# Weight buffers in slots of 16 KB and 8 KB instead of eleven of 8 KB, with gate and up of an expert in one slot

## The chip, the cores and the metric

The kernel runs on one core of a Trainium2 chip. The metric is the device time of one launch in microseconds (us). Three runs before the change took 1690.86, 1692.18 and 1693.26 us; the median is 1692.18. A trace is one further execution under the profiler.

## The reference

The program is a block of two transformer layers over 256 latent tokens and 256 context tokens of width 1024. Each layer modulates its input by a conditioning vector, mixes tokens (layer 0: Fourier groups beside grouped-query attention; layer 1: neighbourhood attention with the context), normalizes, and then runs a mixture of experts. Layer 0 feeds 512 tokens to its experts, layer 1 only the 256 latent ones. What matters here, cut from the reference:

```
scores = jax.nn.sigmoid((h @ w_router).astype(jnp.float32))
_, idx = lax.top_k(scores + e_bias.astype(jnp.float32), TOP_K)     # 8 of 64 experts
...
def expert_block(args):
    tok, e = args
    xb = h_pad[tok]
    a = jax.nn.silu(xb @ w_gate[e]) * (xb @ w_up[e])               # 1024 -> 256, twice
    return a @ w_down[e]                                           # 256 -> 1024
...
routed = jnp.zeros((n_tok + 1, d), h.dtype).at[slot_tok].add(y)[:n_tok]
shared = (jax.nn.silu(h @ s_gate) * (h @ s_up)) @ s_down
return routed + shared
```

Every expert has 1 MB each of gate, up and down weights in float32. All 64 are read in both layers, whatever the routing.

## The kernel before, in words

An expert layer is a list of **jobs** of 128 slots (rows of tokens) each, cut into lanes of 32 columns of the array. A job holds one to three experts: a pair has two, a t in layer 1 has three (`"ptptspt3ptpt3ptptspt3ptptp"`, L77, one letter a job after the first two), an s one expert whose products are formed with its weights split in two parts (`gate_up3`, `down3`). Layer 0 has 43 jobs; a t there is two jobs that share an expert. Layer 1 has 28. A job is worked as gate_up (the token rows against gate and up, L1331 in layer 0 and L1324 in layer 1), an activation, a transposition, down (L1342), and a scatter. On TensorE and SP the order is the order of the code (`manual_schedule`); the other engines are filled in by a scheduler.

**Tokens.** In layer 0, tokens of a job are fetched by an indirect DMA on POOL (`gather`, L1432). The results go back in one of two ways: for the jobs of the range `sent` (L1200) POOL adds them by an accumulating indirect DMA to two arrays accd in HBM (`send`, L1503); the others are placed by matmuls against a one-hot matrix (`scatter`, L1521). Near the end of layer 0, `fetch` (L1510) reads accd back through SP as tiles named ad. `fold` (L1406) joins the sums with the residual and gives the function that adds late scatters.

**Weights.** All weights are loaded by SP in program order, so a load whose slot is still in use holds back everything queued behind it. Slots come from a pool; a slot is free again when the last reader of its tile has ended:

```
def w8(shape, name="w8", dt=F32):
    return wp.tile(shape, dt, name=name, tag="w8", bufs=11)
```

The eleven slots of 8 KB per partition hold, in turn, the modulation weights, the mixers' weights (`halves`, `load_wm`, `kv`), the shared expert (`sh`) and the experts. In layer 0, `load_gu` (L1039) makes two tiles of one expert, each with four of the eight row blocks of gate and up side by side, by four DMAs of 512 KB; one matmul gives gate and up in 512 columns. In layer 1 it makes a gate tile and an up tile, by one DMA of 1 MB each, and `gate_up` (L1318) first runs all gate matmuls (256 columns), then all up matmuls. `experts` (L1068) loads all first tiles of a job's new experts, then all second ones, then the downs. Some down weights of layer 1 go to other pools as dn and dnx (L1063). The first three experts of layer 0 and four of layer 1 are loaded before the routing is known (`static`); the rest are chosen by a register that SP loads from `ordi`.

The last job of layer 1 (`last_job`, L1575) runs gate, then pieces of the scatter, then up.

Of the kernel before, what the change touches and what calls it, by code (L numbers as in the profile page):

```python
# [114 lines left out]
def tile_block(ctx: ExitStack, tc: tile.TileContext, I, out):  # L115
# [79 lines left out]
    def load_wm(k):  # L195

        wm[k] = [w8([128, 4, 2, 256]) for _ in range(2)]
# [646 lines left out]
    def mixer_na(mp):  # L844
# [17 lines left out]
        def fill(n, steps):  # L862
# [8 lines left out]
            kv[n] = [w8([128, 4, 512], "kv") for _ in range(2)]  # L871
# [122 lines left out]
    def norm_h2(l, t, ps, rw_, mp):  # L994
# [17 lines left out]
        S.dma_start(h2d[t * 128:t * 128 + 128, :], hp.rearrange("t j p -> t (j p)"))  # L1012
# [21 lines left out]
    def moe(l, out_of, nt, mp, pre=lambda: None, post=lambda: None):  # L1034
# [4 lines left out]
        def load_gu(e, hs=(0, 1)):  # L1039

            if l:
                w = [w8([128, NJ, FF]) for _ in hs]
                for h, o in zip(hs, w):
                    S.dma_start(o, I[("moe_w_gate", "moe_w_up")[h]][l, e].rearrange("o (p j) n -> p (o j) n", j=NJ))
                return w
            w = [w8([128, 2, 4, FF]) for _ in hs]
            for h, o in zip(hs, w):
                for q, nm in enumerate(("moe_w_gate", "moe_w_up")):
                    S.dma_start(o[:, q], I[nm][l, e].rearrange("o (p j) n -> p (o j) n", j=NJ)[:, 4 * h:4 * h + 4])
            return w  # L1050

# [148 lines left out]
        sent = range(3, njob - 4, 2) if l == 0 else ()  # L1200
# [117 lines left out]
        def gate_up(xT, ws, segs, mid=lambda: None):  # L1318
            p = bank()
            if l:  # L1320
                for q in range(2):
                    for j in range(NJ):
                        for k, sl, kw in segments(segs):
                            T.matmul(p[sl, q * FF:q * FF + FF], xT(j, sl), ws[k][0][q][:, j], start=j == 0,  # L1324
                                     stop=j == NJ - 1, **kw)
# [669 lines left out]
```

## Time and profile before

| | |
|---|---|
| median of three runs | 1692.18 us (1690.86 to 1693.26) |
| the profiled execution's own time | 1695.05 us |
| its span in the trace | 1693.3 us |
| TensorE busy | 1572.6 us, 93% |
| VectorE, ScalarE, GpSimd busy | 784.8, 452.0, 162.9 us |
| mean granted TensorE clock | 0.977 |
| moved by SP's queue | 510.16 MB |
| moved by POOL's queue | 37.81 MB |

The expert jobs of layer 0 stand from about 290 to 955 us, the mixer of layer 1 to about 1150, the experts of layer 1 from 1191 to about 1660. A stage is read by three columns: how much of it TensorE is busy, what clock it was granted, and how busy the DMA engines were. Where TensorE is full and DMA is not, the stage is as long as its matmuls; where DMA is full and TensorE is not, as long as its loads.

### The profile page before, as it was taken

What the parts mean: (1) busy time and instruction counts of PE and PEld (TensorE: products, weight loads), DVE (VectorE), ACT (ScalarE), POOL (GpSimd) and SP (SyncE); (2) the same over time, 40 slices, a digit from 0 to 9 for tenths busy, and PEclk for the clock granted to TensorE, in tenths of its full rate; (3) what the DMA queues carried; (4) which work ended last, traced back from release to release, by engine and by line L of the source; (5) the groups of instructions that cost most, each with busy time, mean ns of one, the idle gap of its engine ahead of it and who ended that gap; (6) DMA issues with size and microseconds to landing.
All of it is one profiled execution on the core that took longest, in us unless ns stands there. A gap on an engine that the chain in (4) does not pass through costs nothing. (4 is left out here: it accounts for less than half of the span.)

```text
span 1693.3 us, 27425 instructions
## 1 busy us (share of the span) xinstructions
PE 1572.6 (93%) x10238; PEld 928.5 (55%) x10238; DVE 784.8 (46%) x2118; ACT 452.0 (27%) x896; POOL 162.9 (10%) x148
## 2 busy tenths in 40 slices
PE   5999999999999999999979799999999998989984
PEld 3765687445445444444434577856656555555542
DVE  2465594356556544435256733347343422223225
ACT  2456311113223223223121333331221211112111
POOL 1003200012111121112200100011000000000001
PEclk9999999999999999999989899999999999999998
DMA  9948866779999999999979855256879999999992
GB/s 328 331 162 299 299 215 212 267 271 371 363 395 341 400 387 398 387 337 389 355 283 408 313 207 199 100 209 262 326 295 420 418 419 419 419 419 419 420 419 107
DMA packets 140808, 549.76 MB, mean 325 GB/s; under 512 B 14288, under 2 KB 23008, under 8 KB 109056
## 3 DMA queue, kind: packets, MB, share of 16 engines
q1 hardware_dynamic: 128368, 510.16, 77.0%
q0 software_dynamic: 12304, 37.81, 7.6%
q8 instruction: 82, 1.34, 0.3%
q14 instruction: 54, 0.44, 0.1%
HBM read 532.63 MB, written 21.05 MB: 327 GB/s over the span
## 5 line engine op out<-in xcount | busy, mean ns | idle before, releaser
L1331 PE MATMUL bank<-w,xT 128*32 128x512 f32 (+2 forms) x1488 | 254.0, 602 | 4.2 <-DMA w<-in_moe_w_up_dram 4.2
L1324 PE MATMUL bank<-w,xT 128*32 128x256 f32 (+2 forms) x2560 | 220.1, 395 | 29.1 <-DMA w<-in_moe_w_up_dram 25.4
L1342 PE MATMUL bank<-w,aT 128*32 128x512 f32 (+2 forms) x1232 | 234.6, 597 | 2.0 <-ACT aT L1298 2.0
L1279 DVE SCALAR_TENSOR_TENSOR a<-s,wsl,bank 128x256 f32<-128x256 f32 x71 | 34.1, 480 | 415.3 <-ACT s L1278 415.3
L1324 PEld LDWEIGHTS bank<-w,xT 128*32 128x32 f32 (+2 forms) x2560 | 130.9, 124 | 116.4 <-DMA w<-in_moe_w_up_dram 33.9
L1521 PE MATMUL bank<-yy,ss 128*128 128x512 f32 x624 | 177.6, 410 | 1.3 <-DVE yy L157 1.0
L1278 ACT ACTIVATE s<-bank 128x256 f32<-128x256 f32 x71 | 27.3, 385 | 544.2 <-PE bank L1331 278.7
L1513 DVE TENSOR_TENSOR acc<-acc,bank 128x512 f32<-128x512 f32 x228 | 149.5, 683 | 45.5 <-PE bank L1521 42.8
L1331 PEld LDWEIGHTS bank<-w,xT 128*32 128x32 f32 (+2 forms) x1488 | 78.6, 125 | 161.0 <-issue 155.0
L1342 PEld LDWEIGHTS bank<-w,aT 128*32 128x32 f32 (+2 forms) x1232 | 67.8, 124 | 120.0 <-issue 106.1
L1521 PEld LDWEIGHTS bank<-yy,ss 128*128 128x128 f32 x624 | 107.4, 190 | 22.5 <-DVE yy L157 2.7
L157 DVE TENSOR_TENSOR yy<-bank,yy 128x512 fp32r<-128x512 f32 x104 | 71.4, 688 | 89.8 <-ACT yy L157 89.8
L157 ACT CAST yy<-bank 128x512 fp32r<-128x512 f32 x104 | 60.9, 586 | 176.6 <-PE bank L1342 158.8
L1432 POOL DMA_INDIRECT xg<-h2d,idx x43 | 51.5, 1198 | 418.4 <-DVE acc L1513 216.8
L157 DVE TENSOR_TENSOR wl<-half,wh 128x1024 fp32r<-128x1024 f32 x35 | 42.7, 1224 | 70.8 <-ACT wh L157 70.8
L1235 DVE TENSOR_SCALAR oh<-ib,pos 128x64 bf16<-128x64 bf16 (+3 forms) x428 | 68.7, 241 | 12.1 <-PE bank L1262 12.0
L161 PE MATMUL bank<-wh,hT 128*128 128x512 f32 x160 | 65.7, 411 | 2.7 <-ACT wh L157 2.1
L162 PE MATMUL bank<-wh,hT 128*128 128x512 f32 x160 | 63.5, 397 | 0.3 <-DVE hT L157 0.2
L163 PE MATMUL bank<-wl,hT 128*128 128x512 f32 x160 | 63.6, 397 | 0.0
L1472 PE MATMUL bank<-ohr,h2p 128*128 128x256 f32 x448 | 60.8, 289 | 0.0
L1472 PEld LDWEIGHTS bank<-ohr,h2p 128*128 128x128 f32 x448 | 55.3, 190 | 8.6 <-PE bank L1324 4.8
L1503 POOL DMA_INDIRECT accd<-yd,idx x32 | 50.2, 1569 | 96.7 <-issue 90.7
(366 smaller groups left out, 2287.7 us busy)
## 6 DMA issues: line engine op xcount, KB each, us to landing
w<-in_moe_w_down_dram SPq DMA_DIRECT2D x104, 1024.0 KB
w<-in_moe_w_gate_dram SPq DMA_DIRECT2D x128, 512.0 KB
w<-in_moe_w_up_dram SPq DMA_DIRECT2D x128, 512.0 KB
w<-in_moe_w_gate_dram SPq DMA_DIRECT2D x64, 1024.0 KB
w<-in_moe_w_up_dram SPq DMA_DIRECT2D x64, 1024.0 KB
w<-in_w_mod_dram SPq DMA_DIRECT2D x24, 1024.0 KB
half<-in_na_w_in_dram SPq DMA_DIRECT2D x12, 1024.0 KB
mh<-in_w_mod_dram SPq DMA_DIRECT2D x12, 1024.0 KB
```

The source lines that it names most:

```text
L157: return A.copy(o_h, src), eng.tensor_sub(o_l, src, o_h.bitcast(F32))
L161: T.matmul(p, xh, wh, start=first, stop=False)
L162: T.matmul(p, xl, wh, start=False, stop=False)
L163: T.matmul(p, xh, wl, start=False, stop=last)
L1235: V.tensor_scalar(oh[:, 32 * lane:32 * (lane + m)], ib[:, off:off + 32 * m], pos[:, t, c:c + 1], None, op0=OP.is_equal)
L1324: T.matmul(p[sl, q * FF:q * FF + FF], xT(j, sl), ws[k][0][q][:, j], start=j == 0, stop=j == NJ - 1, **kw)
L1331: T.matmul(p[sl], xT(j, sl), ws[k][0][j // 4][:, :, j % 4, :], start=j == 0, stop=j == NJ - 1, **kw)
L1342: T.matmul(p[sl], aT[:, j, sl], d[:, n * 512:n * 512 + 512], start=j == 0, stop=j == 1, **kw)
L1432: G.indirect_dma_start(out=x, out_offset=None, in_=h2d[:n2, :], in_offset=bass.IndirectOffsetOnAxis(ap=idx_col, axis=0), bounds_check=n2 - ...
L1472: T.matmul(o, h2p[t][k][:, 2 * q + j], oh[:, t].rearrange("p a b -> p (a b)")[:, :n], start=t == 0 and k == 0, stop=t == nt - 1 and k == 1)
L1513: add = {0: lambda t, r, p: V.tensor_add(acc[t][:, r], acc[t][:, r], p)}
L1521: T.matmul(p, ss[:, t * 128:t * 128 + 128], yy[:, q, r], start=k == 0 and q == 0, stop=k == len(grp) - 1 and q == 1)
```

## The change

The pool of weight slots becomes four of 16 KB and three of 8 KB per partition. A 16 KB slot holds the gate and up weights of one expert (`gu`), or two halves of a mixer's weights, or the shared expert's gate and up. Both layers load an expert's gate and up by two DMAs of 1 MB and run gate_up with 512 columns. Down weights, modulation weights and biases stay in the 8 KB slots. The last job keeps gate before up, as `gate_then_up`. Besides: the write of h2d moves from SP to POOL, the range `sent` ends two jobs earlier (job 37 is scattered by matmuls), and `fold` treats only the latent tokens, with late context sums added to acc by VectorE.

```diff
     def w8(shape, name="w8", dt=F32):
-        return wp.tile(shape, dt, name=name, tag="w8", bufs=11)
+        return wp.tile(shape, dt, name=name, tag="w8", bufs=3)
+
+    def w16(shape, name="w16", dt=F32):
+
+        w = wp.tile([128, 2] + shape, dt, name=name, tag="w16", bufs=4)
+        return [w[:, 0], w[:, 1]]
 
     def halves(name="half", dt=F32):
 
-        return [w8([128, 4, 512], name, dt) for _ in range(2)]
+        return w16([4, 512], name, dt)
...
-        S.dma_start(h2d[t * 128:t * 128 + 128, :], hp.rearrange("t j p -> t (j p)"))
+        G.dma_start(h2d[t * 128:t * 128 + 128, :], hp.rearrange("t j p -> t (j p)"))
...
+        def load_gu(e):
+
+            w = wp.tile([128, 2, NJ, FF], F32, name="gu", tag="w16", bufs=4)
+            for q in range(2):
+                load_half(w, q, e)
             return w
+
+        def load_half(w, q, e):
+            S.dma_start(w[:, q], I[("moe_w_gate", "moe_w_up")[q]][l, e].rearrange("o (p j) n -> p (o j) n", j=NJ))
...
-            for c in new:
-                have[c] = [[], None]
-            for h in range(2):
-                for c, e in zip(new, es):
-                    have[c][0].extend(load_gu(e, (h,)))
+            for c, e in zip(new, es):
+                have[c] = [load_gu(e), None]
...
-        sh = []
-        for nm in ("sh_w_gate", "sh_w_up"):
-            w = w8([128, NJ, FF])
+        sh = w16([NJ, FF], "sh")
+        for w, nm in zip(sh, ("sh_w_gate", "sh_w_up")):
             S.dma_start(w, I[nm][l].rearrange("(p j) n -> p j n", j=NJ))
-            sh.append(w)
...
-        sent = range(3, njob - 4, 2) if l == 0 else ()
+        sent = range(3, njob - 6, 2) if l == 0 else ()
...
-                    T.matmul(p[sl], xT(j, sl), ws[k][0][j // 4][:, :, j % 4, :], start=j == 0, stop=j == NJ - 1, **kw)
+                    T.matmul(p[sl], xT(j, sl), ws[k][0][:, :, j, :], start=j == 0, stop=j == NJ - 1, **kw)
...
-            for t in range(nt):
-                V.tensor_mul(acc[t], acc[t], g2s[t // 2])
+            for t in range(2):
+                V.tensor_mul(acc[t], acc[t], g2s[0])
                 V.tensor_add(xt[t], xt[t], acc[t])
             g2c.extend(g2s[1:])
-            first = set()
 
             def add_x(t, r, p):
                 if t > 1:
-                    if (t, r.start) in first:
-                        return V.tensor_add(acc[t][:, r], acc[t][:, r], p)
-                    first.add((t, r.start))
-                    if r.start == 0:
-                        acc[t] = k4([128, D], "accx")
-                    return A.copy(acc[t][:, r], p)
+                    return V.tensor_add(acc[t][:, r], acc[t][:, r], p)
                 tmp = k2([128, 512], "tmp")
                 V.tensor_mul(tmp, p, g2s[0][:, r])
-                (G if r.start else V).tensor_add(xt[t][:, r], xt[t][:, r], tmp)
+                (G if l and r.start else V).tensor_add(xt[t][:, r], xt[t][:, r], tmp)
...
-                n_grp = 1 if sent and 2 < j < njob - 4 else GRP
+                n_grp = 1 if sent and 2 < j < njob - 6 else GRP
```

In the rows below, a row is one instruction that SP issues, in order; the names are the tile written and the array read, with buffer numbers, and "waits" names the semaphores it stands for: PE_49 is TensorE's count, a DMAHW or DMASW one an earlier DMA's.

First, SP at the start of layer 0's experts, before: the shared expert's weights stand ahead of the token tiles x0 to x3.

```order
L1090 DMA w8_1801<-in_sh_w_gate_dram 128x2048 [waits DMAHW4_49,DMAHW1_49,PE_49]
L1080 DMA cst_1793<-in_cols0_dram 128x128 [waits DMASW0_49,DVE_49,DMASW1_49,Activation_49,Pool_49]
L1082 DMA jm_1795<-in_jmask0_dram 128x129
L1086 DMA rb_1799<-in_moe_bias_dram 128x64
L1090 DMA w8_1803<-in_sh_w_up_dram 128x2048 [waits DMAHW2_49,PE_49]
L1084 DMA rw_1797<-in_moe_w_router_dram 128x512
L1054 DMA w8_1805<-in_sh_w_down_dram 128x2048 [waits DMAHW3_49,PE_49]
L213 DMA x0_1843<-in_x_dram 128x1024
```

And now:

```order
L1056 DMA w8_1793<-in_sh_w_down_dram 128x2048 [waits DMAHW4_49,DMAHW1_49,PE_49]
L1079 DMA cst_1782<-in_cols0_dram 128x128 [waits DMASW0_49,DVE_49,DMASW1_49,Activation_49,Pool_49]
L1081 DMA jm_1784<-in_jmask0_dram 128x129
L1085 DMA rb_1788<-in_moe_bias_dram 128x64
L218 DMA x0_1831<-in_x_dram 128x1024
L1083 DMA rw_1786<-in_moe_w_router_dram 128x512 [waits PE_49]
L218 DMA x1_1889<-in_x_dram 128x1024 [waits DMAHW2_49]
L218 DMA x2_1974<-in_ctx_dram 128x1024 [waits DMAHW3_49,PE_49,Activation_49]
L218 DMA x3_2078<-in_ctx_dram 128x1024 [waits DMAHW4_49,DMASW2_49,DVE_49]
L1088 DMA sh_1790<-in_sh_w_gate_dram 128x2048 [waits DMAHW5_49,PE_49]
L1088 DMA sh_1790<-in_sh_w_up_dram 128x2048 [waits DMAHW6_49]
```

Gate and up of the shared expert have moved behind the token tiles, into one tile sh, and the gate waits for TensorE there; the down weights stay in front.

Second, SP in the last pair job that stands ahead of the first ad, before: half tiles, then two downs, then ad, then the next (split) expert.

```order
L1049 DMA w8_7734<-in_moe_w_gate_dram 128x1024 [waits DMAHW3_49,PE_49]
...
L1049 DMA w8_7734<-in_moe_w_up_dram 128x1024 [waits DMAHW4_49]
...
L1049 DMA w8_7743<-in_moe_w_up_dram 128x1024 [waits DMAHW2_49]
...
L1054 DMA w8_7746<-in_moe_w_down_dram 128x2048 [waits DMAHW3_49,PE_49]
...
L1054 DMA w8_7748<-in_moe_w_down_dram 128x2048 [waits DMAHW4_49,PE_49]
L1510 DMA ad_7828<-accd0_77 128x1024 [waits DMAHW5_49,DMASW7_49,DMASW1_49]
L1510 DMA ad_7831<-accd1_78 128x1024 [waits DMAHW6_49,DMASW2_49]
...
L1049 DMA w8_7843<-in_moe_w_gate_dram 128x1024 [waits DMAHW7_49,PE_49]
...
L1049 DMA w8_7843<-in_moe_w_up_dram 128x1024 [waits DMAHW0_49]
```

And now, at the same place:

```order
L1052 DMA gu_7547<-in_moe_w_gate_dram 128x2048 [waits DMAHW7_49]
...
L1052 DMA gu_7547<-in_moe_w_up_dram 128x2048 [waits DMAHW0_49]
...
L1052 DMA gu_7550<-in_moe_w_gate_dram 128x2048 [waits DMAHW1_49,PE_49]
...
L1052 DMA gu_7550<-in_moe_w_up_dram 128x2048 [waits DMAHW2_49]
...
L1056 DMA w8_7553<-in_moe_w_down_dram 128x2048 [waits DMAHW3_49,PE_49]
...
L1056 DMA w8_7555<-in_moe_w_down_dram 128x2048 [waits DMAHW4_49,PE_49]
L1504 DMA ad_7635<-accd0_76 128x1024 [waits DMAHW5_49,DMASW1_49]
L1504 DMA ad_7638<-accd1_77 128x1024 [waits DMAHW6_49,DMASW5_49,DMASW2_49]
...
L1052 DMA gu_7650<-in_moe_w_gate_dram 128x2048 [waits DMAHW7_49]
...
L1052 DMA gu_7650<-in_moe_w_up_dram 128x2048 [waits DMAHW0_49]
```

Two whole experts take four DMAs of twice the size; the pair's second down (w8_7555) waits for TensorE directly ahead of ad, and the expert behind is gu_7650.

Third, SP at the start of layer 1's experts, before: three static experts after the first, with an h2d write between.

```order
L1044 DMA w8_10194<-in_moe_w_gate_dram 128x2048 [waits DMAHW3_49]
L1044 DMA w8_10195<-in_moe_w_up_dram 128x2048 [waits DMAHW4_49,PE_49]
L1054 DMA dn_10198<-in_moe_w_down_dram 128x2048 [waits DMAHW5_49]
L1044 DMA w8_10200<-in_moe_w_gate_dram 128x2048 [waits DMAHW6_49,PE_49]
L1044 DMA w8_10201<-in_moe_w_up_dram 128x2048 [waits DMAHW7_49,PE_49]
L1054 DMA dn_10204<-in_moe_w_down_dram 128x2048 [waits DMAHW0_49]
L1044 DMA w8_10206<-in_moe_w_gate_dram 128x2048 [waits DMAHW1_49,PE_49]
L1044 DMA w8_10207<-in_moe_w_up_dram 128x2048 [waits DMAHW2_49,PE_49]
L1054 DMA dn_10210<-in_moe_w_down_dram 128x2048 [waits DMAHW3_49]
L1012 DMA h2d_122<-hp_10239 128x1024 [waits DMAHW4_49,DVE_49]
```

And now:

```order
L1052 DMA gu_9698<-in_moe_w_gate_dram 128x2048 [waits DMAHW1_49,PE_49]
L1052 DMA gu_9698<-in_moe_w_up_dram 128x2048 [waits DMAHW2_49]
L1056 DMA dn_9701<-in_moe_w_down_dram 128x2048 [waits DMAHW3_49]
L1052 DMA gu_9976<-in_moe_w_gate_dram 128x2048 [waits DMAHW4_49,PE_49]
L1052 DMA gu_9976<-in_moe_w_up_dram 128x2048 [waits DMAHW5_49]
L1056 DMA dn_9979<-in_moe_w_down_dram 128x2048 [waits DMAHW6_49]
L1052 DMA gu_9981<-in_moe_w_gate_dram 128x2048 [waits DMAHW7_49,PE_49]
L1052 DMA gu_9981<-in_moe_w_up_dram 128x2048 [waits DMAHW0_49]
L1056 DMA dn_9984<-in_moe_w_down_dram 128x2048 [waits DMAHW1_49]
L1052 DMA gu_9986<-in_moe_w_gate_dram 128x2048 [waits DMAHW2_49,PE_49]
L1052 DMA gu_9986<-in_moe_w_up_dram 128x2048 [waits DMAHW3_49]
L1056 DMA dn_9989<-in_moe_w_down_dram 128x2048 [waits DMAHW4_49]
```

The four static experts stand in the same order, gate and up of each in one tile; the gate of each waits for TensorE once, the up no more, and the h2d write is gone from this queue.

## Rows read from the trace of the kernel before

**Rows 1.** The page, busy time of the engines: us, share of span, instructions.
```profile
PE 1572.6 (93%) x10238; PEld 928.5 (55%) x10238; DVE 784.8 (46%) x2118; ACT 452.0 (27%) x896; POOL 162.9 (10%) x148
```
**Rows 2.** Windows: stretch, us, each engine's busy us (instructions), PEclk, DMA share, GB/s.
```profile
400.00:800.00 400.00, 386.79 (x2378) 188.19 (x2377) 208.17 (x514) 112.10 (x192) 72.84 (x53) 1.00 1.00 377
...
1192.00:1253.00 61.00, 57.86 (x488) 36.00 (x485) 23.27 (x102) 13.59 (x25) 0.00 (x0) 1.00 0.80 318
1253.00:1655.00 402.00, 372.93 (x3425) 222.16 (x3425) 116.80 (x349) 73.34 (x143) 0.00 (x0) 0.98 1.01 418
```
**Rows 3.** The page's groups of gate_up: count | busy us, mean ns | idle before.
```profile
L1331 PE MATMUL bank<-w,xT 128*32 128x512 f32 (+2 forms) x1488 | 254.0, 602 | 4.2 <-DMA w<-in_moe_w_up_dram 4.2
L1324 PE MATMUL bank<-w,xT 128*32 128x256 f32 (+2 forms) x2560 | 220.1, 395 | 29.1 <-DMA w<-in_moe_w_up_dram 25.4
```
**Rows 4.** Waits of TensorE, 800 to 960 us: total us, times, longest.
```profile
PE bank L161 <- ACT wh L157: 5.4, 1, 5.4
...
PE bank L1331 <- DMA w<-in_moe_w_up_dram: 4.2, 3, 2.6
```
**Rows 5.** Waits of TensorE, 1190 to 1670 us.
```profile
PE bank L1324 <- DMA w<-in_moe_w_up_dram: 25.4, 16, 2.3
```
**Rows 6.** SP's issues, 186 to 200 us: start us, us, engine line op, tiles.
```profile
188.15 0.34 SPq L1090 DMA_DIRECT2D w<-in_sh_w_gate_dram  x1
...
191.68 0.33 SPq L1090 DMA_DIRECT2D w<-in_sh_w_up_dram  x1
```
**Rows 7.** TensorE, 241 to 254 us: start us, us, line, tiles, count.
```profile
242.72 0.39 PE L163 MATMUL bank<-wo,yT 128*128 128x512 f32 x1
...
244.68 7.13 PE L1379 MATMUL bank<-w,h2T 128*128 128x256 f32 x32
```
**Rows 8.** TensorE, 812 to 829 us: two jobs' gate_up and a down.
```profile
813.83 7.08 PE L1331 MATMUL bank<-w,xT 128*32 128x512 f32 x64
...
827.52 1.94 PE L1331 MATMUL bank<-w,xT 128*64 128x512 f32 x8
```
**Rows 9.** SP's issues, 820 to 900 us.
```profile
847.51 2.38 SPq L1510 DMA_DIRECT2D ad<-accd  x2
...
851.25 0.34 SPq L1049 DMA_DIRECT2D w<-in_moe_w_up_dram  x1
...
868.73 0.81 SPq L1510 DMA_DIRECT2D ad<-accd  x2
```
**Rows 10.** TensorE, 833 to 862 us.
```profile
837.65 3.65 PE L1342 MATMUL bank<-w,aT 128*64 128x512 f32 x16
...
848.51 1.18 PE L1521 MATMUL bank<-yy,ss 128*128 128x512 f32 x4
...
860.29 0.80 PE L161 MATMUL bank<-wh,xT 128*128 128x512 f32 x1 [5.42 <-ACT wh L157]
```
**Rows 11.** ScalarE, 853 to 863 us.
```profile
859.19 1.99 ACT L157 CAST wh<-w 128x1024 fp32r<-128x1024 f32 x2 [3.69 <-DMA w<-in_moe_w_up_dram]
```
**Rows 12.** Windows: the stretch right after that wait (columns of rows 2).
```profile
860.29:865.50 5.21, 5.17 (x11) 3.64 (x12) 4.70 (x4) 2.88 (x3) 0.00 (x0) 0.50 0.47 197
```
**Rows 13.** TensorE, 876 to 888 us.
```profile
881.10 7.33 PE L1331 MATMUL bank<-w,xT 128*32 128x512 f32 x44 [2.62 <-DMA w<-in_moe_w_up_dram]
```
**Rows 14.** VectorE, 932 to 946 us, one of the four L1410 adds.
```profile
937.74 1.22 DVE L1410 TENSOR_TENSOR xr<-xr,acc 128x1024 f32<-128x1024 f32 x1
```
**Rows 15.** SP's issues, 1145 to 1200 us.
```profile
1161.07 0.42 SPq L1054 DMA_DIRECT2D dn<-in_moe_w_down_dram  x1
...
1192.10 0.35 SPq L1054 DMA_DIRECT2D w<-in_moe_w_down_dram  x1
```
**Rows 16.** TensorE, 1191 to 1215 us: gate_up of layer 1's first two jobs.
```profile
1191.29 14.03 PE L1324 MATMUL bank<-w,xT 128*64 128x256 f32 x128
```
**Rows 17.** SP's issues, 1196 to 1262 us: x2 stands for two in one row.
```profile
1226.75 17.62 SPq L1044 DMA_DIRECT2D w<-in_moe_w_gate_dram  x2
```

More of the change, by code (lines that the diff above doesn't have):

```diff
@@ L195, in load_wm @@
     def load_wm(k):
-        wm[k] = [w8([128, 4, 2, 256]) for _ in range(2)]
+        wm[k] = w16([4, 2, 256], "wm")
         for h in range(2):
@@ L870, in fill @@
                 A.activation(qT[n][:, i], ps[i][:, :256], AF.Copy, scale=SCALE)
-            kv[n] = [w8([128, 4, 512], "kv") for _ in range(2)]
+            kv[n] = w16([4, 512], "kv")
             ps = project(na[2 + n], channel_major(h, 512), tick, nxt=lambda: na[4 + n])
@@ L1037, in moe @@
         NS = pl.ahead
[L1039 to L1049, printed above, removed]
-            return w
+        def load_gu(e):
+            w = wp.tile([128, 2, NJ, FF], F32, name="gu", tag="w16", bufs=4)
+            for q in range(2):
+                load_half(w, q, e)
+            return w
+        def load_half(w, q, e):
+            S.dma_start(w[:, q], I[("moe_w_gate", "moe_w_up")[q]][l, e].rearrange("o (p j) n -> p (o j) n", j=NJ))
         def load_dn(d_ap, tile=w8):
@@ L1316, in segments, with gate_up, gate_then_up @@
             return out
-        def gate_up(xT, ws, segs, mid=lambda: None):
+        def gate_up(xT, ws, segs):
             p = bank()
[L1320 to L1325, printed above, removed]
-                    if q == 0:
-                        mid()
-                return p
             for j in range(NJ):
                 for k, sl, kw in segments(segs):
-                    T.matmul(p[sl], xT(j, sl), ws[k][0][j // 4][:, :, j % 4, :], start=j == 0, stop=j == NJ - 1, **kw)
+                    T.matmul(p[sl], xT(j, sl), ws[k][0][:, :, j, :], start=j == 0, stop=j == NJ - 1, **kw)
+            return p
+        def gate_then_up(xT, ws, segs, mid):
+            p = bank()
+            for q in range(2):
+                for j in range(NJ):
+                    for k, sl, kw in segments(segs):
+                        T.matmul(p[sl, q * FF:q * FF + FF], xT(j, sl), ws[k][:, q, j], start=j == 0,
+                                 stop=j == NJ - 1, **kw)
+                if q == 0:
+                    mid()
             return p
@@ L1352, in gu_parts @@
                 wh, wl = k4(shape, "wh", F32R), k4(shape, "wl", F32R)
-            split(wh, wl, w[0][jj // 4][:, :, jj % 4:jj % 4 + 2], V)
+            split(wh, wl, w[0][:, :, jj:jj + 2], V)
             return wh, wl
@@ L1575, in last_job @@
             es = [ds(S.value_load(ordi[0:1, sg_[0]:sg_[0] + 1], min_val=0, max_val=NE - 1), 1) for sg_ in segs]
-            wgu = [[], []]
-            for h in range(2):
+            wgu = [wp.tile([128, 2, NJ, FF], F32, name="gu", tag="w16", bufs=4) for _ in es]
+            for q in range(2):
                 for w, e in zip(wgu, es):
-                    w.extend(load_gu(e, (h,)))
+                    load_half(w, q, e)
             wd = [w8([128, 2, D]) for _ in es]
@@ L1590, in two_pieces @@
                 next(sc)
-            p = gate_up(xT, [[w] for w in wgu], segs, two_pieces)
+            p = gate_then_up(xT, wgu, segs, two_pieces)
             for _ in sc:
```

## The prediction

> **What bounds the kernel now.** I read the engine line first: TensorE is busy for 1572.6 us of 1693.3 [rows 1]. That alone would say that only TensorE work counts, so I next read the stages [rows 2]. From 400 to 800 us (layer 0's experts) TensorE is busy for 386.79 us of 400 and the DMA engines are at 1.00 as well, at 377 GB/s: two resources are full at once and neither has slack for the other. From 1253 to 1655 us (layer 1's experts) the DMA share is 1.01 at 418 GB/s and TensorE has idle time. The waits agree: in layer 1, L1324 waits 25.4 us for weights in 16 pieces [rows 5], while layer 0's whole tail has one large wait, 5.4 us at L161, and 4.2 us at L1331 [rows 4]. So the reader is to see a kernel that lives on weights being loaded far ahead, and in layer 1 one that is as long as its weight stream. The change rearranges the buffers that hold this lead. The bytes of buffer stay 88 KB per partition; what differs is that seven slots, not eleven, are handed back, and gate and up of an expert together.
>
> **The change, part by part.** The sum is made against the profiled execution, 1695.05 us (span 1693.3 and 1.75 around it); the median of the runs is 2.87 lower, and I take that off at the end. 1 MB below is 1024 KB, 1.049 million bytes, so 2.51 us at 418 GB/s.
>
> *Matmul form.* In layer 1, 256-column matmuls become 512-column ones. L1331 spends 254.0 us on 1488 x 512 columns, L1324 220.1 us on 2560 x 256 [rows 3]: 0.333 and 0.336 ns a column, so 1.6 us of TensorE time is saved, in a stretch that waits for DMA. I count 0. The covering work is the weight stream; if it were gone, the gain would be 1.6.
>
> *Entry of layer 0, about +4.5 (0 to 6.5).* Before, the shared expert's gate and up were queued at 188 to 192 us [rows 6], some 50 us before L1379 reads them at 244.68 [rows 7]. Now all four 16 KB slots hold the output projection of the mixer until its last matmul, 242.72 + 0.39 = 243.1 [rows 7], and only then SP can issue the gate. It needs 2.51 us of transfer and a latency. The nearest row for that: the half expert queued at 851.25 reached ScalarE at 859.19, 7.9 us later, with 2.1 million bytes (5.0 us) to move from the first ad read before it [rows 9, 11], so at most 2.9 us. 243.1 + 2.5 + 2.6 = 248.2, against 244.68: 3.5 us of waiting. The up half follows 2.5 us later and is needed after half of the 7.13 us. I add 1 for the modulation streams, which now share three slots (0 to 2). The x loads and h2d writes change queue or place by a few microseconds and are waited for by nobody at the edge; 0.
>
> *Steady layer 0, about +7 (0 to 31).* A pair job lasts 13.69 us, 813.83 to 827.52 [rows 8], and brings six tiles, 15.1 us of DMA. A job with two new experts is short by 1.36 us, and the lead pays for it. With three down slots, SP now stands at a pair's second down load until the down matmuls of the job before have ended (the second fence of order rows on the tail shows such a PE wait just ahead of ad); behind it stand the next gate and up. Eight jobs of layer 0 bring two new experts right after a job that did: 8 x 1.36 = 10.9. Some of it is still covered, since two whole experts are loaded: I take 7. The lower end is that all is covered, as it is now; the upper counts the 0.5 MB gather and 0.5 MB scatter of each such job too, 8 x (1.36 + 2.5).
>
> *Tail of layer 0, about +4.5 (-5 to +9).* Before, SP stood until 847.51 at the read of ad, for an accumulating scatter that is now not sent; the split expert behind it was issued at 850 and TensorE waited 5.42 us at 860.29 [rows 9, 10]. That reason goes. What is late next: the second down load of the pair ahead of ad waits for the down matmuls that ended at 837.65 + 3.65 = 841.3 [rows 10]. From there two downs, two ad reads (0.5 MB each) and the gate and up, 5 MB or 12.6 us with what is in flight, and the latency give 856 to 858, against 854.9, when TensorE is free: a wait of about 2.4, so -3. The next job's weights are still issued behind the standstill to 868.73 [rows 9]; now its first matmuls want 4 MB, where half an expert each was enough. Two ad and 4 MB from 868.73 are 12.6 us, with latency 884, where the gate_up now goes through its last wait at 881.10 [rows 13]: +3.5. Sixteen more scatter matmuls, at 1.18 us for four [rows 10], less what overlaps: +4. -3 + 3.5 + 4 = +4.5.
>
> *Vector work at the end of layer 0: 0 (-2 to +2).* Two L1410 adds of 1.22 us leave the chain [rows 14], four adds of a bank to acc take their place.
>
> *Entry of layer 1 and its stream, about +14 (1.5 to 24).* Before, four static experts were queued by 1161.07 and SP took up the routed ones at 1192.10 [rows 15]; their weights fed 14.03 us of gate_up without a gap from 1191.29 [rows 16]. Now the fourth expert's gate and up need a slot that is freed only by the end of the first gate_up, 1191.29 + 14.03 / 2 = 1198.3, and the down loads that went at 1192.10 stand behind them. So the stream starts 6.2 us later and with 3 MB (7.5 us) still to bring: 13.7 us. From 1253 on, DMA is full at 1.01 [rows 2], so this lag reaches the end one for one. TensorE's own wait for the fourth expert, 5.0 us of transfer and a latency, lies inside it. Between 1192 and 1253 the DMA share is 0.80: 12.2 us are idle, around SP's standstill from 1226.75 to 1244 [rows 2, 17]. If all of it were taken up, 1.5 remains; if the third down slot adds about 10 us of standing there, 24. I expect one to replace the other.
>
> Sum: 4.5 + 7 + 4.5 + 0 + 14 = 30. 1695.05 + 30 = 1725; less 2.87, **1722**.
>
> **Two rules against the rows.** Layer 0 loads in pieces of 512 KB at 377 GB/s beside gathers and scatters, layer 1 in pieces of 1 MB at 418 [rows 2]. The Trainium skill, "DMA: Bandwidth & Descriptors", section on measured bandwidth, says to batch transfers to 1 MiB or more; by that rule layer 0's stream would come nearer to 418, the +7 would vanish and the time be 1715. After 5.42 us without work TensorE ran at 0.50 of its clock, 1.2 GHz, from 860.29 to 865.5 [rows 10, 12]. The Trainium skill, "TensorE: Matmul & The Clock Gate", section on HAM oscillation, tells of just this after waits for DMA; by it each new wait as long as that one costs 2.6 us more, and if three of mine were that long the sum would be 1730.
>
> **The rivals.**
> 1. *The lead is enough in layer 0.* For it: now TensorE waits almost nowhere there, and the bytes of buffer are the same. Against it: a DMA share of 1.00 over 400 us. Without the steady +7 and with half of the entry and tail (4.5), 1695.05 + 18.5 - 2.87 = 1711.
> 2. *Faster.* The one mechanism is the tail's standstill at ad: if its end lets the split expert and the next job load in time, the 5.4 and 4.2 us of waits and 2.6 us of half clock go [rows 4, 12], 12.2 in all, against 4 for the scatter matmuls: 1692.18 - 8.2 = 1684. It decides only if layer 1's stream also catches up its lag between 1198 and 1253, where it has 12.2 idle us for 13.7.
> 3. *The ring of four starves layer 1 all along.* A gate slot now comes free at the end of a gate_up, 3.5 us later than before (half of 7.0). Ten jobs of layer 1 have three experts and need a fifth slot with the next job. If half of the 3.5 is not covered each time, 10 x 1.75 = 17.5 us more: 1740. Against it: down loads are queued between, and keep the engines busy meanwhile.
> 4. *Nothing to be measured*: loss and gain cancel, 1692. No row speaks for a balance so exact.
>
> **How the numbers follow.** The forecast has 0.58, rival 1 has 0.18, rival 2 has 0.07, rival 3 has 0.14, rival 4 has 0.03. 0.2% (3.4 us) is about what a measurement of this kernel can tell from no change. All cases but rivals 2 and 4 are slower by more: 0.90; faster 0.07; the same 0.03. The forecast's own terms, none at its end, give 1710 to 1735; with rival 1 below and most of rival 3 above, the range is 1704 to 1738.
>
> **What would show it.** Right: a TensorE wait of 2 to 5 us at the shared expert's first matmul near 245; SP standing at down loads in layer 0, waits at gate_up on up weights; no 5.4 us wait at L161 but one of 2 to 3; a wait of about 6 us at layer 1's second gate_up; the DMA share from there to the end again 1.0 at 418 GB/s, but ending some 14 us later relative to layer 1's start. Wrong: layer 0 without DMA waits at gate_up (then rival 1), a first weight of the fourth expert that is issued before the first gate_up ends, or bubbles in the DMA share after 1270 (then rival 3).

## The result and the profile after

The changed kernel takes 1740.95 us (median of four, 1739.17 to 1743.61) against 1692.72 of the kernel before beside it: ratio 1.0286, interval 1.0272 to 1.03. It is 48.2 us slower, outside the range that was forecast (1704 to 1738). Its profiled execution has a span of 1739.2 us, 45.9 more than before.

The page's busy line answers [rows 1]: TensorE is busy for 26 us more, although it has 1236 instructions fewer.

```profile
PE 1598.8 (92%) x9002; PEld 886.1 (51%) x9002; DVE 786.0 (45%) x2118; ACT 451.4 (26%) x893; POOL 159.1 (9%) x150
```

Fixed stretches of time, as in [rows 2], hold other work in the two kernels, so I cut both traces at the same five instructions: a transposition in an early job of layer 0, a product of a split expert near its end, one of layer 1's mixer, a transposition of its routing, and a gather product further on (a matmul that fetches a job's tokens); the last stretch ends 17.1 us before the end of either span. A "..." stands for the mixer. Columns are those of rows 2. Before, the stretches are the steady part of layer 0, its tail, the start of layer 1's experts, and the rest of them:

```profile
321.30:797.00 475.70, 461.37 (x2848) 226.59 (x2846) 246.60 (x636) 132.46 (x228) 85.45 (x62) 1.00 0.97 362
797.00:961.40 164.40, 142.02 (x745) 69.83 (x743) 88.09 (x127) 40.24 (x71) 16.16 (x14) 0.93 0.90 337
...
1177.30:1343.00 165.70, 162.53 (x1428) 102.75 (x1427) 67.19 (x286) 35.34 (x66) 0.00 (x0) 0.99 0.86 348
1343.00:1676.20 333.20, 299.98 (x2667) 175.67 (x2666) 96.72 (x239) 61.38 (x119) 3.30 (x2) 0.97 0.96 398
```

The same work in the changed kernel:

```profile
325.83:819.46 493.63, 470.40 (x2844) 232.19 (x2843) 246.50 (x632) 132.80 (x228) 85.30 (x62) 0.98 0.91 349
819.46:984.82 165.36, 146.31 (x760) 75.15 (x758) 87.82 (x131) 37.17 (x66) 9.27 (x10) 0.92 0.88 343
...
1200.20:1388.60 188.40, 171.91 (x996) 84.41 (x995) 67.14 (x286) 35.30 (x66) 0.00 (x0) 0.96 0.82 335
1388.60:1722.10 333.50, 302.68 (x1851) 139.96 (x1850) 96.68 (x239) 61.40 (x119) 3.30 (x2) 0.96 0.95 390
```

Read the second column, the length. The entry gives 325.83 - 321.30 = +4.5, the steady part +17.9, the tail +1.0, the mixer 1200.20 - 1177.30 less what was there at 984.82 - 961.40, -0.5, the start of layer 1 +22.7, the rest +0.3: together 45.9. Two places carry 40.6 of it. In the steady part, half is idle TensorE (475.70 - 461.37 = 14.3 before, 23.2 now: +8.9) and half is the same matmuls running longer (+9.0), at a mean granted clock of 0.98 where it was 1.00. The DMA engines, at 0.97 before, are at 0.91. The start of layer 1 divides in the same way: +13.3 of idle time (3.17 before, 16.49 now) and +9.4 of longer matmuls, at 0.96 for 0.99.

The queue of loads tells why. SP's longest waits in layer 0 (400 to 860, the steady part and the first of the tail; total, times, longest), L1056 the downs and L1052 gate and up:

```profile
SPq L1056 <- PE bank L1342: 126.7, 13, 14.9
SPq L1056 <- PE bank L1259: 115.8, 11, 15.6
SPq L1056 <- DVE wl L162: 62.8, 7, 12.4
SPq L1052 <- PE bank L1319: 29.0, 9, 5.7
```

Before (400 to 850), the longest of those for TensorE, L1054 the downs and L1049 gate and up:

```profile
SPq L1054 <- PE bank L1331: 59.2, 15, 13.3
SPq L1049 <- PE bank L1331: 39.4, 23, 3.4
...
SPq L1049 <- PE bank L1262: 29.3, 8, 4.7
SPq L1049 <- PE bank L1342: 27.8, 8, 4.5
```

Before, SP stood for a slot for 88 us at the downs in all (59 in the row shown) and for about 100 at gate and up; now it stands for 305 us at the downs, with the next gate and up behind them, and for 35 at gate and up. TensorE meets this as a handful of new waits of 1.3 to 2.6 us: some 5 us more at split experts, whose weights need a copy (L162) before the product, and 3.9 us in two waits of pair jobs for up weights. One of the first kind and the granted clock with it, first on TensorE's timeline (in brackets the idle time ahead):

```profile
528.99 0.50 PE L166 MATMUL bank<-wh,xT 128*128 128x512 f32 x1 [1.37 <-ACT wh L162]
...
530.77 0.80 PE L168 MATMUL bank<-wl,xT 128*128 128x512 f32 x1 [1.04 <-DVE wl L162]
...
533.92 0.63 PE L166 MATMUL bank<-wh,xT 128*128 128x512 f32 x1
```

And the stretch at half clock in the windows:

```profile
530.10:536.90 6.80, 6.13 (x14) 4.81 (x15) 4.01 (x4) 1.68 (x2) 0.00 (x0) 0.50 1.02 425
```

The clock fell to 0.50, 1.2 GHz, at 530.1, within the second of two waits of 1.37 and 1.04 us, both shorter than the 5.42 of [rows 10, 12]. There are five such stretches between 400 and 800, 20 us in all; before there was one of 3.4 us. By an estimate from these numbers, 20 us at half the clock lose some 10 us of matmul time and the 3.4 before lost 1.7, which is most of the +9.0. Not every such wait does this: one of 1.65 us in the same kernel left the clock at 1.00.

```profile
612.84 0.50 PE L168 MATMUL bank<-parts,xT 128*128 128x512 f32 x1 [1.65 <-DVE parts L162]
```
```profile
612.84:619.00 6.16, 5.78 (x29) 4.56 (x29) 4.21 (x6) 3.49 (x6) 5.09 (x3) 1.00 1.03 412
```

The entry, SP and then TensorE [rows 6, 7]: the shared expert's gate is issued only when the output projection is all but done (its last matmul starts at 243.07), and its first product waits.

```profile
242.57 0.33 SPq L1088 DMA_DIRECT2D sh<-in_sh_w_gate_dram  x1
```
```profile
247.99 8.20 PE L1379 MATMUL bank<-sh,h2T 128*128 128x256 f32 x24 [2.39 <-DMA sh<-in_sh_w_gate_dram]
```

The tail of layer 0, SP and TensorE [rows 9, 10, 13]: the standstill is now at the downs ahead of ad, the 5.42 us wait has become 1.63, and the next job waits 6.3 us in two waits, where it waited 4.2 in three [rows 4].

```profile
850.09 14.69 SPq L1056 DMA_DIRECT2D w<-in_moe_w_down_dram  x2
864.89 0.96 SPq L1504 DMA_DIRECT2D ad<-accd  x2
866.63 0.34 SPq L1052 DMA_DIRECT2D gu<-in_moe_w_gate_dram  x1
```
```profile
879.61 0.50 PE L166 MATMUL bank<-wh,xT 128*128 128x512 f32 x1 [1.63 <-ACT wh L162]
...
899.33 1.93 PE L1319 MATMUL bank<-gu,xT 128*32 128x512 f32 x6 [3.29 <-DMA gu<-in_moe_w_up_dram]
904.31 2.74 PE L1319 MATMUL bank<-gu,xT 128*32 128x512 f32 x9 [3.05 <-DMA gu<-in_moe_w_up_dram]
```

The start of layer 1 [rows 15, 16]: SP takes the fourth expert's gate only at 1221.38, 7.1 us into the first gate_up, and the second gate_up waits. Over the whole layer TensorE's waits on up weights are 39.7 us, against the 25.4 of [rows 5], to which 3.6 for gates come. The surplus is all in the start: 13.3 us of such waits there, where there was none before.

```profile
1186.83 0.58 SPq L1056 DMA_DIRECT2D dn<-in_moe_w_down_dram  x1
1221.38 0.33 SPq L1052 DMA_DIRECT2D gu<-in_moe_w_gate_dram  x1
```
```profile
1214.27 7.94 PE L1319 MATMUL bank<-gu,xT 128*64 128x512 f32 x34
1228.80 7.56 PE L1319 MATMUL bank<-gu,xT 128*64 128x512 f32 x24 [6.58 <-DMA gu<-in_moe_w_up_dram]
```
```profile
PE bank L1319 <- DMA gu<-in_moe_w_up_dram: 39.7, 13, 6.6
```

### The profile page after: what moved, and what is told of

It reads as the page before. It is cut to its first block, busy times and chain, and to the rows that moved or that the text cites. A ratio compares the mean times of both kernels' runs of the same rounds, so it can differ in the third digit from the quotient of the medians.

```text
span 1739.2 us, 24323 instructions
## 1 busy us (share of the span) xinstructions
PE 1598.8 (92%) x9002; PEld 886.1 (51%) x9002; DVE 786.0 (45%) x2118; ACT 451.4 (26%) x893; POOL 159.1 (9%) x150
## 5 line engine op out<-in xcount | busy, mean ns | idle before, releaser
L1319 PE MATMUL bank<-gu,xT 128*32 128x512 f32 (+2 forms) x2736 | 481.1, 626 | 49.9 <-DMA gu<-in_moe_w_up_dram 49.9
L1319 PEld LDWEIGHTS bank<-gu,xT 128*32 128x32 f32 (+2 forms) x2736 | 153.5, 127 | 346.1 <-issue 328.1
L1515 PE MATMUL bank<-yy,ss 128*128 128x512 f32 x640 | 181.3, 410 | 1.9 <-DVE yy L162 1.6
L162 DVE TENSOR_TENSOR yy<-bank,yy 128x512 fp32r<-128x512 f32 x106 | 72.8, 688 | 94.0 <-ACT yy L162 94.0
L162 ACT CAST yy<-bank 128x512 fp32r<-128x512 f32 x106 | 61.9, 585 | 184.3 <-PE bank L1342 167.0
L162 DVE TENSOR_TENSOR wl<-half,wh 128x1024 fp32r<-128x1024 f32 x35 | 42.6, 1223 | 70.8 <-ACT wh L162 70.8
L1232 DVE TENSOR_SCALAR oh<-ib,pos 128x64 bf16<-128x64 bf16 (+3 forms) x428 | 68.5, 239 | 13.0 <-PE bank L1259 12.8
L1440 PEld LDWEIGHTS bank<-head,xg 128*128 128x128 f32 x344 | 39.5, 142 | 28.7 <-issue 26.8
L1440 PE MATMUL bank<-head,xg 128*128 128x128 f32 x344 | 53.2, 278 | 0.0
## 6 DMA issues: line engine op xcount, KB each, us to landing
gu<-in_moe_w_up_dram SPq DMA_DIRECT2D x128, 1024.0 KB, 13.9
```

The lines of the kernel that those rows point to most:

```text
L162: return A.copy(o_h, src), eng.tensor_sub(o_l, src, o_h.bitcast(F32))
L1232: V.tensor_scalar(oh[:, 32 * lane:32 * (lane + m)], ib[:, off:off + 32 * m], pos[:, t, c:c + 1], None, op0=OP.is_equal)
L1319: T.matmul(p[sl], xT(j, sl), ws[k][0][:, :, j, :], start=j == 0, stop=j == NJ - 1, **kw)
L1440: T.transpose(p[:, j * 128:j * 128 + 128], x[:, (q * 4 + j) * 128:(q * 4 + j) * 128 + 128], ident)
L1515: T.matmul(p, ss[:, t * 128:t * 128 + 128], yy[:, q, r], start=k == 0 and q == 0, stop=k == len(grp) - 1 and q == 1)
```

## The experiments

**The queue changes alone.** On the kernel before: h2d from POOL, the shorter range `sent`, the new `fold`; the eleven slots stay.

```diff
-        S.dma_start(h2d[t * 128:t * 128 + 128, :], hp.rearrange("t j p -> t (j p)"))
+        G.dma_start(h2d[t * 128:t * 128 + 128, :], hp.rearrange("t j p -> t (j p)"))
...
-        sent = range(3, njob - 4, 2) if l == 0 else ()
+        sent = range(3, njob - 6, 2) if l == 0 else ()
...
```

> The kernel before with only the other parts of the change: h2d written by POOL, the sent jobs ending two earlier, the shorter fold. Eleven slots of 8 KB stay. Theory (the slots alone cost the 48 us): SP no longer stands at ad until 847, so most of the 5.4 us wait at the split job goes, for 4 us of scatter matmuls: 1687 to 1692. Rival (these parts carry some of the loss): 1697 or more.

1692.48 us, ratio 0.9994 (0.9982 to 1.0006): no difference that can be measured, and just above the range of the theory (1687 to 1692). Together these parts carry none of the loss; it belongs to the slots and what goes with them. That the parts cancel each other is shown by the last run below.

**Layer 0: the downs behind the next gate and up.** The changed kernel, with SP's order in layer 0 turned: before a job's downs, the next job's gate and up are queued.

```diff
...
+                if l == 0:
+                    gate_ups([sg_[0] for sg_ in segs])
+                    if j + 1 < njob:
+                        gate_ups([sg_[0] for sg_ in jobs[j + 1]])
+                    downs([sg_[0] for sg_ in segs])
...
```

> The changed kernel, in layer 0 with one other order on SP: gate and up of the next job are queued ahead of the down weights of this one. Theory A (in layer 0 SP standing at the three down slots holds back the next gate and up, and the waits and half clock come from that): the lag against before at the end of layer 0's steady part falls from about 22 us to 8 to 12, the end to 1726 to 1732. Rival B (four slots of gate and up, or the bandwidth beside gathers and scatters, are the limit): 1738 to 1745, with waits for down weights instead.

1723.43 us, ratio to before 1.0174 (1.0153 to 1.0194): 17.5 less than the changed kernel, more than the theory asked. The lag at the end of the steady part fell less than it asked, from 22.5 to 15.7 us instead of 8 to 12, in part because this trace entered the steady part 3.7 us later than the changed kernel's; the tail gave the rest. The two stretches of layer 0:

```profile
329.51:812.69 483.18, 464.34 (x2843) 230.46 (x2841) 247.99 (x635) 132.34 (x228) 81.81 (x62) 0.99 0.95 364
812.69:966.12 153.43, 138.59 (x760) 72.21 (x760) 86.69 (x128) 38.74 (x67) 9.09 (x9) 0.97 0.92 360
```

The steady part loses 7.5 us against before where it lost 17.9, and the tail is 11.0 shorter than before: with gate and up ahead of the standstill the waits of [rows 4] go as well. SP stands no shorter in this run, 398 us from 321 to 835 against 391 in the changed kernel:

```profile
SPq L1052 <- PE bank L1333: 283.7, 28, 17.6
```

but now mostly at gate and up. So the standing by itself was not the cost; what was queued behind it was.

**A fourth 8 KB slot, and its control.** Room for a fourth slot comes from the pool of 4 KB tiles; the control has that cut alone.

```diff
-NK4 = 13
+NK4 = 11
...
-        return wp.tile(shape, dt, name=name, tag="w8", bufs=3)
+        return wp.tile(shape, dt, name=name, tag="w8", bufs=4)
```

> Control for the next run: the changed kernel with the pool of 4 KB tiles cut from 13 to 11 buffers, to make room for one more 8 KB slot. Theory: these buffers are spare, 1739 to 1744. Rival (they are needed): over 1746.

> The changed kernel with a fourth 8 KB slot (and the pool of 4 KB tiles cut as in the control). Theory (layer 0's loss is SP standing for a down slot of the ring of three, with the next gate and up behind it): layer 0 regains most of what the other order of loads gave, so 10 to 17 us less than the control. Rival (a ring of four hands a pair's slots back just as late, because the same down matmuls free them two by two): within 5 us of the control.

The control takes 1810.5 us (1.0689, 1.0665 to 1.0712): its rival was right, those tiles are needed (42.9 us late at 961, 114 at the end). So only the difference counts: with the slot 1790.78 us (1.0575, 1.0559 to 1.0592), 19.7 less, somewhat more than the 10 to 17 of the theory. The steady part of layer 0, the control first, then with the fourth slot:

```profile
336.25:831.95 495.70, 470.35 (x2844) 232.31 (x2842) 247.60 (x632) 133.39 (x228) 85.78 (x62) 0.98 0.91 349
```
```profile
336.31:818.16 481.85, 461.80 (x2843) 226.14 (x2842) 247.20 (x632) 133.29 (x228) 85.77 (x62) 1.00 0.95 363
```

The control has the changed kernel's loss here (495.70 against 493.63), and one slot takes 13.9 us of it away, most of the 9 us of longer matmuls among them (470.35 to 461.80). By size and by order the same cause is shown: the ring of three down slots holds back gate and up. Neither repair takes all: 6 to 7.5 us stay in the steady part. With the fourth slot nearly all of them are idle time (20.05 us against 14.33 before). No run shows what they come from; four slots for gate and up, or loads of 1 MB where there were 512 KB, are untested rivals.

**Layer 1: gates in one slot, ups in another.** The changed kernel, with two experts' gates loaded into one 16 KB slot and their ups into the next, and all gate matmuls ahead of the ups, 256 columns each.

```diff
...
+                w = [wp.tile([128, 2, NJ, FF], F32, name="gu", tag="w16", bufs=4) for _ in range(2)]
+                for q in range(2):
+                    for k, (c, e) in enumerate(cc):
+                        S.dma_start(w[q][:, k], I[("moe_w_gate", "moe_w_up")[q]][l, e].rearrange(
+                            "o (p j) n -> p (o j) n", j=NJ))
...
```

> The changed kernel, in layer 1 with one slot for two experts' gates and one for their ups, gates loaded and multiplied first (256 columns), so that a slot is handed back after half a gate_up. Number and size of slots stay. Theory A (the 9 us that the stream of layer 1 loses after its late start come from slots that are handed back 3.5 us later): DMA share back to 1.0 from 1276 on, 1730 to 1734. Rival B (four slots of 16 KB are too few in either form): 1738 to 1745.

1728.19 us (1.0206, 1.0191 to 1.0222), 12.8 less than the changed kernel and below both ranges. It changes two things at once, the slots' contents and the form of the matmuls, which the next run parts.

**Layer 1: the matmul form alone.** Slots and loads as in the changed kernel; only the matmuls are 256 columns wide, gates first.

```diff
         def gate_up(xT, ws, segs):
+            if l:
+                return gate_then_up(xT, [w[0] for w in ws], segs, lambda: None)
```

> The changed kernel with its slots and loads untouched; only layer 1's matmuls are 256 columns wide again, all gates and then all ups. Theory A (what the kernel with gates and ups in separate slots gained came from matmuls that start before the up half has landed): 1727 to 1732, and L1 waits of TensorE on up much shorter. Theory B (it came from slots that are handed back after the gates): 1739 to 1743.

1729.46 us (1.022, 1.0201 to 1.024), 11.5 less: nearly all of what the run before gained is the form; that slots come back earlier is worth about 1.3, no more than the runs' own spread. In its trace 1.7 of the 11.0 us of the span were there already when layer 1's experts began. The start of layer 1 is 7.7 us shorter than in the changed kernel, and 15.0 longer than before:

```profile
1198.50:1379.20 180.70, 168.37 (x1428) 107.44 (x1427) 67.19 (x286) 35.30 (x66) 0.00 (x0) 0.97 0.84 340
```

The second gate_up waits 4.55 us there and not 6.58, since its gates can begin without the ups; all waits for weights in the start are 9.2 us for 13.3, and the rest of the 7.7 are matmuls that ran longer (171.91 to 168.37). Over the whole layer TensorE waits for weights nearly as long as in the changed kernel, 37.2 us against 39.7, now for gates and not for ups; the gain is at the start.

**Both repairs.** The late downs of layer 0 and the separate slots of layer 1 in one kernel.

> The changed kernel with both repairs: layer 0 queues the next job's gate and up ahead of this job's downs, and layer 1 puts the gates of two experts in one slot, their ups in another, gates first. Theory (two separate losses, each handed on to the end one for one): 1740.95 - 17.5 - 12.8 = 1710.6, so 1708 to 1714. Rival (layer 1's stream has time of its own to catch up, so that layer 0's loss is partly hidden there and the two gains overlap): 1716 to 1723.

1710.51 us (1.0106, 1.0084 to 1.0127), against 1710.6 by addition: layer 1 hides nothing of what layer 0 loses.

**The fourth fixed expert in 8 KB slots.** The kernel with both repairs, and the expert for which no 16 KB slot is free gets two of the small ones; one routed down is no longer loaded early, to make room.

```diff
+                gu = load_gu8(slice(c, c + 1)) if l and c == 3 else load_gu(slice(c, c + 1))
...
-                for c in range(NS, NS + 2):
+                for c in range(NS + 1, NS + 2):
```

> As the kernel with both repairs, and besides layer 1's fourth fixed expert has its gate and up in two of the 8 KB slots (the early load of one routed down goes, and is queued after its job's gates). Theory (the fourth expert stood for a 16 KB slot until the first gate_up's end, and that late start of layer 1's stream reaches the end): TensorE's wait of some 6 us at the second gate_up goes and the time falls by 5 to 8 against the kernel with both repairs. Rival (the standstill only moves, to the next routed gate or down): within 2 us of the kernel with both repairs.

1704.57 us (1.0076, 1.0057 to 1.0095), 5.9 less. The start of layer 1 with both repairs, then with this one too, and its first gate_ups, which run through as in [rows 16]:

```profile
1181.60:1359.70 178.10, 166.11 (x1428) 103.96 (x1427) 67.21 (x286) 35.28 (x66) 0.00 (x0) 0.97 0.85 344
```
```profile
1180.40:1351.70 171.30, 164.26 (x1427) 103.12 (x1427) 67.20 (x286) 35.29 (x66) 0.00 (x0) 0.98 0.88 358
```
```profile
1194.47 14.03 PE L1356 MATMUL bank<-gu,xT 128*64 128x256 f32 x128
```

6.8 us less in this stretch, and 5.9 of it at the end: the fourth expert's late start is handed on nearly one for one.

**The entry of layer 0.** The last kernel, with the shared expert's gate and up in 8 KB slots too, early, and h2d from SP in layer 0.

```diff
+        sh = w16([NJ, FF], "sh") if l else [w8([128, NJ, FF], "sh") for _ in range(2)]
...
+        (G if l else S).dma_start(h2d[t * 128:t * 128 + 128, :], hp.rearrange("t j p -> t (j p)"))
```

> As the kernel with both repairs and the fourth fixed expert in 8 KB slots, and besides in layer 0 the shared expert's gate and up in two 8 KB slots, early, and h2d written from SP again. Theory (the entry's lag of 6 to 9 us at 320 is the shared expert's weights and the h2d writes, and reaches the end): 6 to 9 us below the 1704.57 of that kernel, 1695 to 1699. Rival (the lag is regained anyway at the end of layer 0, where that kernel had 3 of its 13 us left): 1702 to 1706.

1698.98 us (1.0044, 1.0028 to 1.006), 5.6 less. The job at 321.30 before starts at 319.28, where the last kernel had it at 327.94: of these 8.7 us two thirds reach the end. The run undoes two things, and does not say how much of the lag is the late gate and how much the h2d writes. All repairs of the ring together come to 0.4% above the kernel before, not below it; against the last run below, which has the same end of layer 0 and the eleven slots, it is 11.9 us.

**512 columns in layer 1 of the kernel before.** Eleven slots, but each holds half the row blocks of gate and up, in pieces of 512 KB, as in layer 0.

```diff
...
-            if l:
+            if l and whole:
...
-        def gate_up(xT, ws, segs, mid=lambda: None):
+        def gate_up(xT, ws, segs, mid=None):
...
-            if l:
+            if mid:
...
```

> The kernel before with layer 1's gate_up in 512 columns, its weights in two tiles of 8 KB that each hold half of gate and half of up, as in layer 0; the last job keeps gate before up. Theory (layer 1 lives on its weight stream, the form of the matmul is worth nothing either way): 1690 to 1695. Rival (512 columns delay by themselves, since a matmul needs gate and up of a half): 1700 or more.

1704.13 us (1.0072, 1.0058 to 1.0085): 11 to 12 us slower, and the theory that the form costs nothing is wrong. Two causes are mixed here, which the next run parts.

**512 KB pieces alone.** The kernel before, with each of layer 1's gate and up loads cut in two.

```diff
-                    S.dma_start(o, I[("moe_w_gate", "moe_w_up")[h]][l, e].rearrange("o (p j) n -> p (o j) n", j=NJ))
+                    for i in (0, 4):
+                        S.dma_start(o[:, i:i + 4],
+                                    I[("moe_w_gate", "moe_w_up")[h]][l, e].rearrange("o (p j) n -> p (o j) n", j=NJ)[:, i:i + 4])
```

> The kernel before, with layer 1's gate and up weights loaded by two DMAs of 512 KB each in place of one of 1 MB; tiles, slots and matmuls as before. Theory A (the 512-column run lost 11 us because its matmuls need both halves of gate and up at once): 1691 to 1695. Theory B (it lost them to the smaller transfers, 411 for 418 GB/s): 1699 to 1705.

1697.87 us (1.0041, 1.0028 to 1.0055): some 7 us slower, between the two ranges. Of the 11 to 12 us the pieces are some 7, the form the remaining 4 or 5. The DMA view of 1253 to 1655, before and with the smaller pieces:

```profile
DMA packets 25296, 168.16 MB, mean 418 GB/s; under 512 B 2788, under 2 KB 2788, under 8 KB 6661
```
```profile
DMA packets 39640, 165.18 MB, mean 411 GB/s; under 512 B 4399, under 2 KB 4399, under 8 KB 34609
```

402 us at 411 for 418 is 6.7 us, and the run lost some 7: here the full stream lost about what its rate lost. The cut halves two things, the transfer and the run of bytes per partition (8 KB to 4 KB); which of them lowers the rate is not shown.

**The end of layer 0 alone.** The kernel before, with the range `sent`, the grouping and `fold` of the change, and h2d still from SP.

```diff
-        sent = range(3, njob - 4, 2) if l == 0 else ()
+        sent = range(3, njob - 6, 2) if l == 0 else ()
...
-                n_grp = 1 if sent and 2 < j < njob - 4 else GRP
+                n_grp = 1 if sent and 2 < j < njob - 6 else GRP
```

> The kernel before with the changes at the end of layer 0 alone (the range of sent jobs, the fold), h2d still written from SP. Theory (in the run with all queue changes the h2d writes from POOL cost the 6 us by which it was late at 321, and the end of layer 0 gave them back): 1685 to 1688, faster than both kernels. Rival (the gain at the end is only there to be had after a delay, because DMA then has less to catch up): 1690 to 1693.

1687.11 us (median of five; ratio 0.9963, 0.9949 to 0.9976): faster than both kernels. The wait of [rows 10] is 1.63 us here. The first read of ad no longer waits for an accumulating scatter (up to 15.8 us before), so it goes at 827.94 and not at 847.51 [rows 9], and the split expert's weights behind it go at 830.12 and not at 850.73:

```profile
852.78 0.50 PE L161 MATMUL bank<-wh,xT 128*128 128x512 f32 x1 [1.63 <-ACT wh L157]
```
```profile
827.94 1.19 SPq L1504 DMA_DIRECT2D ad<-accd  x2
830.12 0.34 SPq L1049 DMA_DIRECT2D w<-in_moe_w_gate_dram  x1
```

Weights issued 23 us before their first product leave a wait of the same 1.63 us as in the changed kernel, where they were issued 13 us before. So in neither does the load end it, but ScalarE's copy, which goes on without a wait of its own. And the clock, which fell after this pair of waits in the changed kernel (1.63 and 0.76 us), stayed up here, after waits of the same lengths; the changed kernel first:

```profile
881.60:885.10 3.50, 3.50 (x10) 2.45 (x9) 2.86 (x3) 0.80 (x1) 0.00 (x0) 0.51 0.00 0
```
```profile
852.78:859.60 6.82, 6.05 (x26) 4.68 (x27) 4.85 (x5) 2.80 (x3) 0.00 (x0) 1.00 0.00 0
```

In the trace the tail is 2.8 us shorter; a lead of 3.5 us was there at 318 already, before anything that was changed, and other runs with an unchanged entry stood between -1.8 and +2.4 there. So of the 5.4 us of the medians about half is shown at its place. The run with all queue changes, 0.9994, differs from this one by the h2d writes from POOL alone: they cost some 5 us. In that run's trace the routing product at 244.95 waited 1.80 us for h2T, and TensorE was 6.0 us late at 321.

## Why the prediction was wrong

The sign and most of the places were right, the size was 19 us short (1740.95 against 1722). By its steps:

- *Entry, +4.5:* measured +4.5, with the wait that was named: the gate behind the output projection, 2.39 us where 3.5 was worked out, and some idle time and half clock behind it. But the exact number is luck, since kernels with an unchanged entry differ by more than 4 us there. And the h2d writes, counted as 0 in the same term, cost some 5 us in the kernel before: the run with all queue changes was 6.0 late at the same place, with the gate early. The run that undid the lag, worth 5.6 us, took back both, so the share of the late gate is not shown.
- *Steady layer 0, +7:* **the step that failed first**; measured +17.9. The standstill at the pair's second down was named, but its cost was taken as eight jobs' deficit, 10.9 us of transfer, less what the lead covers. (The job list of the kernel has six such jobs, not eight: 8.2 us by the same sum.) Two things were missing. Waits come where the lead is gone, at split experts and at two pair jobs, five of them of 1.3 to 2.6 us: +8.9 of idle time. And five groups of waits took the clock down to 0.50, where one did before: +9.0 of longer matmuls. The rows had shown this [rows 12], and I put it beside the sum, for waits as long as 5.42 us only. The order of loads takes 10.4 of the 17.9 away, the fourth slot 13.9; that some 7 are left, as many as were forecast, says nothing for the deficit, for no run shows what they are. The Trainium skill, "TensorE: Matmul & The Clock Gate", section on HAM oscillation, describes such half-clock work after waits for DMA; the trace agrees in kind, but with waits of 1.37 and 1.04 us, and other waits of that size left the clock up. By it I reckoned 1730, still too little, as I counted three waits.
- *Larger transfers:* the Trainium skill, "DMA: Bandwidth & Descriptors", section on measured bandwidth, advises transfers of 1 MiB or more, and by it the +7 would have vanished. The rate itself agrees (411 GB/s in 512 KB pieces, 418 in 1 MB, in layer 1), but here layer 0's fell from 362 to 349 over the same work, with SP standing. The rate of a transfer is of no use when its slot is not free.
- *Tail, +4.5:* measured +1.0. To the split expert, -3 was worked out and the lag went from 22.5 at 797 to 19.3, -3.1, though not by the late load of the forecast (a wait of 2.4): the 1.63 us left are the copy's. The next job's two waits, 3.29 and 3.05 us, half clock (898.5 to 909, where 879 to 886 was so before) and the scatter took 5.6 back by 894; after that 1.5 was regained.
- *Matmul form, 0:* **the second step that failed.** I counted columns and took the cover of the weight stream for free. But a product over gate and up at once starts when the ups are there, gates alone start a transfer earlier. Undone, the start of layer 1 is 7.7 us shorter and the time 11.5.
- *Layer 1, +14:* with the form undone the start of layer 1 is +15.0, so the size came out; as changed it is +22.7. But the mechanism, a stream that starts late for want of a slot for the fourth expert, was to carry 13.7 us, and the run that gives it another slot took 6.8 away. The rest of the 15.0 has other causes, so the size is in part luck. The late start reaches the end, as was said, because from 1343 on the stream sets the pace: 333.20 and 333.50 us for the same work.

Summed: 10.9 (steady) + 7.7 (form) + 1.0 (layer 1's start) - 3.5 (tail) - 0.2 (the rest) = 15.9, the whole way from the 30 forecast to the trace's 45.9; the medians differ by another 2.3.

Of the rivals, the first, a lead that is enough in layer 0, is refuted by the steady part's +17.9. The third gives the time, 1740, but not by its mechanism: the slots are not late all along, for after the start nothing is lost, and handing them back earlier was worth about 1.3 us. The second, a tail that gains, does exist, but only with the order of loads turned (-11.0) or in the kernel before (-2.8 in the trace).

Left open: the 7 us that stay in layer 0's steady part; the last 5.6 us of layer 1's start (171.30 against 165.70), where four slots of 16 KB still stand against eleven of 8 KB; what the late gate and the h2d writes each cost at the entry; and why the control's 4 KB tiles cost 70 us. None was tried further.

## What to carry to other kernels

The bytes of a buffer are not its lead: count the slots, and ask of every load that can stand what is queued behind it on the same queue. Where a matmul engine is nearly full, a new wait can bring half-clock work with it, also a short one; give that a price of its own in the sum, from rows, and a range, for waits of one size did and did not bring it here. Before widening a product, ask which operand comes last, for the wider product waits for it. And undo a change in its parts: here one small part, at the end of layer 0, was a gain that the rest had hidden.

## What was not expected of the hardware

The clock fell to 0.50 at 530.1, after an idle time of 1.37 us, two matmuls and the first part of another idle time, of 1.04 us. After 1.63 and 0.76 us it fell in one kernel (0.51 from 881.6) and stayed at 1.00 in another (852.78 to 859.6). Cutting loads of 1 MB in two lowered a full stream from 418 to 411 GB/s, with the share of busy DMA engines at 1.02 and most packets under 8 KB (34609 of 39640, against 6661 of 25296), and that 1.7% (6.7 us of 402) was about the whole loss of 7 us.
